# RWKV scan: inverses by 16x16 lanes joined on TensorE, the join handed out over the steps of the running chain

## The chip, the cores and the metric

One core of a Trainium2 chip runs the whole program in one launch. Five engines work side by side, each through its own queue in order: TensorE (PE, with its weight loads PEld), VectorE (DVE), ScalarE (ACT), GpSimd (POOL) and SyncE (SP), which issues the DMAs. They meet through semaphores. The metric is device time of the launch in microseconds (us); less is better.

## The reference

Two layers work on 256 context and 512 latent tokens of width 1024. Layer 0 is windowed attention with an MLP. Layer 1 is a bidirectional RWKV-7 mixer with an MLP. The change touches only the mixer's scan, which is, for 16 heads of 64 channels and for two directions:

```python
def wkv_scan(r, w, k, v, a, b, s0, reverse):
    # S_t = S_{t-1} diag(w_t) + (S_{t-1} a_t) b_t^T + v_t k_t^T ;  y_t = S_t r_t
    def step(s, inp):
        r_t, w_t, k_t, v_t, a_t, b_t = inp
        sa = jnp.einsum('bhvk,bhk->bhv', s, a_t)
        s = s * w_t[:, :, None, :] + sa[..., None] * b_t[:, :, None, :] + v_t[..., None] * k_t[:, :, None, :]
        return s, jnp.einsum('bhvk,bhk->bhv', s, r_t)
s_fwd, yc_fwd = wkv_scan(rc, decc[0], kc, vc, nac, bc, zero, False)   # context first
_, y_fwd = wkv_scan(r, dec[0], k, v, na, b, s_fwd, False)             # latents start from its state
```

The backward direction is the same with `reverse=True`. The outputs are normalised per head, gated, summed and multiplied by `w_o`.

## The kernel before

The scan is done in chunks of 64 tokens. Inside a chunk the recurrence is a triangular system, so per chunk, head and direction the kernel inverts a 64x64 unit triangular matrix, and from chunk to chunk only the 64x64 state is carried.

**Six iterations** (`its`): context for heads 0 to 7 (iteration 0), two latent iterations of four heads each (1, 2), then the same for heads 8 to 15 (3, 4, 5). A context chain has four steps, a latent chain eight. The products of an iteration are in `AR`, `BK` and `GM`, of which there are two sets, used in turn.

**Work of one iteration n.**
- `prep` (by parts of one head pair and direction: four parts for latents, eight for context): loads features, two exponentials on ACT (`en`, `cs`; one buffer for `en`), products `ko`, `bo`, `ao` and, for latents, the one with `r`. Of these `ao` is on DVE (L1201), the others on POOL (L1199, L1200, L1203). Then `grams(..., 0)`: ACT fills `pad`, PE multiplies into `g_ps` (L1224), DVE masks into `GM` (L1230).
- `lanes` (L1264): the two 32x32 diagonal blocks of every triangle are copied to `MT` (two of the four copies on POOL), transposed to `lane`, and inverted by 30 steps of forward substitution on DVE, each step in two or three streams of one product (L1281) and one sum (L1284), on all blocks at once. Each step reads what the step before wrote.
- `merge` (L1286): two transposes on DVE (L1289 to `MT`, L1292 to `dt`), then PE makes the off-diagonal 32x32 block in two rounds, `mg1` (L1299) and `mg2` (L1307), each followed by copies on ACT.
- `late`: the second half of the grams (latents), `to_end` (a product over `BK` on POOL, L1245) and `turn` (32 transposes on PE, L1323).
- `chain` (L1343): per step PE makes `x_ps` (L1368, L1371), ACT copies it to `xsb`, PE makes `u_ps` (L1394), ACT copies it to `z`, PE makes `s_ps` (L1409), and DVE adds it to the state (L1416). The state had been multiplied by its decay before, on POOL (L1387). Latents also make `y_ps` (L1426, L1430). Two groups of heads go through a step one behind the other.
- `readout`: norm, gates and bonus; its products are shared by POOL and DVE (tables `RO`, `RL`).

**Order.** The program is written as: `front(1)`, chain 0, `front(2)`, chain 1, and so on. `front(n)` is `merge(n-1)`, `prep(n)`, `lanes(n)`, and puts `late(n)` into a list `rest`; `after(i)` takes pieces of `rest` behind step i of the running chain, by the tables `LS` and `LC`. So merge n-1 has to be done before chain n-1 begins. A scheduler places all instructions on their engines by priority (earlier in the program first) and by its own estimate of when they are ready; on the chip each engine keeps that order. `prep(0)` and `lanes(0)` run beside the projections ahead of the scan. Merge 0 puts its second transpose into a free part of `GM`, since `dt` lies in memory that opens only behind the projections.

## Time and profile before

| | us |
|---|---|
| median of 3 runs | 2300.29 (2295.81 to 2302.07) |
| profiled execution, its own time | 2301.24 |
| its span, first to last instruction | 2299.5 |
| PE busy | 2052.4 (89%) |
| DVE busy | 1300.0 (57%) |
| ACT busy | 853.0 (37%) |
| POOL busy | 514.4 (22%) |

The scan takes the stretch from about 1389 to 1894 us of the span. In a row of groups the columns are line, engine, operation, output and inputs, shape, count, then busy us and mean ns of one, then idle time of the engine before them and what ended it. In a row of the timeline they are the start, the duration of the merged run, and in brackets the idle time before. An `x128` of PE there counts entries of the trace, of which each f32 matmul with a small tile makes two. PEclk is the granted share of the TensorE clock.

### The profile page before, as it was taken

Reading aid. Unit: us, or ns where it says so; the run is one execution under the profiler, and the core shown is the slowest. Engines: PE = TensorE matmul, PEld = TensorE weight load, DVE = VectorE, ACT = ScalarE, POOL = GpSimd, SP = SyncE. Lnnn points to the kernel's source line nnn. Section 1 sums busy time; section 2 is a strip of 40 time slices with the busy share of each in tenths; the row PEclk is TensorE's granted clock in tenths of the full one; section 3 lists DMA queues with packets and bytes.
Section 4 is the critical chain, followed back from the end, with each engine's and each line's share of the span. In section 5 each row is a group of like instructions: output and inputs, shape, how many; then the busy total and the mean of one; then the engine's idle time right before and its main releaser. Section 6 shows DMA issues by size and latency. Waiting matters only on the chain. (4 is left out here: it accounts for less than half of the span.)

```text
span 2299.5 us, 40632 instructions
## 1 busy us (share of the span) xinstructions
PE 2052.4 (89%) x16208; PEld 1676.3 (73%) x16208; DVE 1300.0 (57%) x2492; ACT 853.0 (37%) x1696; POOL 514.4 (22%) x586
## 2 busy tenths in 40 slices
PE   5989999989999999995989897488767996999999
PEld 4876756868888888884856786376656764788887
DVE  4455564364333343349687464985897747444444
ACT  4345454231111111116454346366655543222121
POOL 1122232010000000003011225537553332101110
PEclk9999999989999999997989898697787997999999
DMA  8244464222212222121245434203221322323322
GB/s 296 88 136 146 156 201 157 74 78 64 65 56 64 65 65 65 51 65 58 84 182 215 147 113 138 61 12 96 77 67 42 112 69 74 101 92 97 96 92 78
DMA packets 115885, 229.67 MB, mean 100 GB/s; under 512 B 12912, under 2 KB 31088, under 8 KB 115312
## 3 DMA queue, kind: packets, MB, share of 16 engines
q1 hardware_dynamic: 115696, 227.08, 30.7%
q8 instruction: 128, 2.10, 0.4%
q14 instruction: 61, 0.50, 0.1%
HBM read 191.80 MB, written 32.60 MB: 98 GB/s over the span
## 5 line engine op out<-in xcount | busy, mean ns | idle before, releaser
L337 DVE TENSOR_TENSOR wlo<-wraw,whi 128x1024 fp32r<-128x1024 f32 (+1 forms) x121 | 134.2, 1118 | 316.7 <-ACT whi L334 170.4
L362 PE MATMUL w_ps<-mhh,whi 128*128 128x512 f32 (+1 forms) x768 | 235.6, 361 | 7.4 <-POOL whi L336 4.0
L364 PE MATMUL w_ps<-mhl,whi 128*128 128x512 f32 (+1 forms) x768 | 235.6, 361 | 5.7 <-DVE mhl L317 5.7
L366 PE MATMUL w_ps<-mhh,wlo 128*128 128x512 f32 (+1 forms) x768 | 235.7, 361 | 4.1 <-DVE wlo L337 4.1
L364 PE MATMUL w_ps<-hid,w2h 128*128 128x512 f32 (+1 forms) x768 | 233.9, 359 | 0.0
L362 PE MATMUL w_ps<-hid,w2h 128*128 128x512 f32 (+1 forms) x768 | 231.1, 355 | 0.6 <-DVE X L709 0.6
L366 PE MATMUL w_ps<-hid,w2l 128*128 128x512 f32 (+1 forms) x768 | 231.1, 355 | 0.0
L336 POOL TENSOR_SCALAR whi<-wraw 128x1024 fp32r<-128x1024 f32 (+1 forms) x60 | 70.6, 1177 | 637.1 <-PE w_ps L364 261.1
L334 ACT ACTIVATE w2h<-w2raw 128x512 fp32r<-128x512 f32 x64 | 40.4, 632 | 331.2 <-PE w_ps L364 292.4
L362 PEld LDWEIGHTS w_ps<-mhh,whi 128*128 128x128 f32 x768 | 128.2, 190 | 32.1 <-POOL whi L336 4.7
L658 DVE SCALAR_TENSOR_TENSOR X<-w_ps,ada,X 128x256 f32<-128x256 f32 (+1 forms) x128 | 73.1, 613 | 137.5 <-PE w_ps L366 137.5
L364 PEld LDWEIGHTS w_ps<-mhl,whi 128*128 128x128 f32 x768 | 127.8, 190 | 31.6 <-DVE mhl L317 8.4
L366 PEld LDWEIGHTS w_ps<-mhh,wlo 128*128 128x128 f32 x768 | 127.7, 190 | 30.2 <-DVE wlo L337 7.2
L366 PEld LDWEIGHTS w_ps<-hid,w2l 128*128 128x128 f32 x768 | 127.4, 189 | 23.3
L334 ACT ACTIVATE whi<-wraw 128x1024 fp32r<-128x1024 f32 (+1 forms) x61 | 59.0, 968 | 225.4 <-PE w_ps L364 106.2
L362 PEld LDWEIGHTS w_ps<-hid,w2h 128*128 128x128 f32 x768 | 125.6, 188 | 22.9 <-issue 1.0
L364 PEld LDWEIGHTS w_ps<-hid,w2h 128*128 128x128 f32 x768 | 126.5, 188 | 20.9
L336 POOL TENSOR_SCALAR w2h<-w2raw 128x512 fp32r<-128x512 f32 x64 | 42.3, 660 | 425.9 <-PE w_ps L364 326.7
L687 ACT ACTIVATE mrelu<-w_ps 128x768 f32<-128x768 f32 (+1 forms) x64 | 44.5, 697 | 187.5 <-PE w_ps L366 187.5
L1224 PE MATMUL g_ps<-pad,bk 128*128 128x128 f32 x640 | 97.0, 306 | 16.3 <-DVE lane L1284 6.5
L1281 DVE TENSOR_TENSOR ltmp<-lane 128x36 f32<-128x36 f32 (+34 forms) x402 | 111.0, 313 | 0.1
L1284 DVE TENSOR_TENSOR lane<-lane,ltmp 128x36 f32<-128x36 f32 (+34 forms) x402 | 105.9, 301 | 0.0
(378 smaller groups left out, 4713.7 us busy)
## 6 DMA issues: line engine op xcount, KB each, us to landing
ada_w<-ada_w SPq DMA_DIRECT2D x192, 256.0 KB, 3.4
wraw<-w SPq DMA_DIRECT2D x64, 512.0 KB, 3.2
w2raw<-w SPq DMA_DIRECT2D x128, 256.0 KB, 2.7
feat<-cs SPq DMA_DIRECT2D x16, 390.0 KB, 2.4
cs<-feat SPq DMA_DIRECT2D x24, 260.0 KB, 3.5
wraw<-wq SPq DMA_DIRECT2D x8, 512.0 KB, 4.0
wraw<-wo SPq DMA_DIRECT2D x8, 512.0 KB, 3.3
wraw<-wkv SPq DMA_DIRECT2D x8, 512.0 KB, 3.4
```

What stands on the lines that cost most here:

```text
L334: nc.scalar.activation(hi, raw, AF.Copy)
L336: nc.gpsimd.tensor_scalar(hi, raw, 1.0, 0.0, ALU.mult, ALU.add)
L337: nc.vector.tensor_tensor(lo, raw, hi.bitcast(F32), ALU.subtract)
L362: nc.tensor.matmul(o, wh, cut(xh, sl), start=start, stop=False)
L364: nc.tensor.matmul(o, wh, cut(xl, sl), start=False, stop=False)
L366: nc.tensor.matmul(o, wl, cut(xh, sl), start=False, stop=stop)
L658: self.nc.vector.scalar_tensor_tensor(self.X[:, m, sl], ps[:, sl], self.ada[:, u, m, s:s + 1], self.X[:, m, sl], ALU.mult, ALU.add)
L687: nc.scalar.activation(r, ps[:, 0:n], AF.Relu)
L1224: nc.tensor.matmul(g[:, P * k:P * k + P], it.BK[:, d, b + k], pv[:, :, k], start=True, stop=True)
L1281: nc.vector.tensor_tensor(tmp, Lt[:, t0:t1, s_:s_ + 1].to_broadcast([P, m, n]), Lt[:, s_:s_ + 1, c0:c1].to_broadcast([P, m, n]), ALU.mult)
L1284: nc.vector.tensor_tensor(x, x, tmp, ALU.add)
```

## The change

**Lanes of 16.** `lanes` inverts the four 16x16 diagonal blocks of a 64x64 triangle in 14 steps instead of 30, in two streams (`q`) of a product and a sum, 56 operations of at most 56 elements per partition. All four copies to `MT` are now on ACT and DVE.

**Join on PE.** `merge` first joins pairs of 16x16 blocks to 32x32: a transpose of the upper half (L1270), a transpose of `lane` to `dt` (L1271), one round of 128 matmuls `mh1` (L1275), two copies on ACT (one of them of the new constant `half`), a second round of 128 matmuls `mh2` (L1283), a copy on ACT (L1284), and a transpose of `dt` to `MT` on DVE (L1285). Then `mg1` and `mg2` follow as before. `DT` is always `dt`.

**Where the merge stands.** `merge(n)` is now the last piece of `rest` of `front(n)`, so it belongs to the last steps of chain n-1; merge 0 stands ahead of `front(1)`. `rest` is shared out evenly over the steps from step 1 on.

**POOL to DVE.** All products of `prep`, `to_end` and `readout` go to DVE. The decay of the state is no longer a separate product: the update is one operation `state * decay + s_ps` on DVE per head pair and direction, 128x128 each (L1402), four per step of a latent chain and eight of a context chain, instead of two additions.

The diff, cut:

```diff
-LS = (0, 0, 1, 1, 1, 1, 1, 0)
-LC = (0, 2, 4, 4)
-TE = "pp"
...
-FC = 'apap'
-BC = 'pvav'
+FC = 'avav'
+BC = 'avav'
...
-                nc.gpsimd.tensor_tensor(ko, kp, en, ALU.mult)
-                (nc.gpsimd if "b" in PM else nc.vector).tensor_tensor(bo, bp, en, ALU.mult)
-                (nc.gpsimd if "a" in PM else nc.vector).tensor_tensor(ao, kk, ep[:, :, exc], ALU.mult)
+                nc.vector.tensor_tensor(ko, kp, en, ALU.mult)
+                nc.vector.tensor_tensor(bo, bp, en, ALU.mult)
+                nc.vector.tensor_tensor(ao, kk, ep[:, :, exc], ALU.mult)
                 if it.lat:
-                    nc.gpsimd.tensor_tensor(ar[:, :, 64:128], src[fl, "r"], ep[:, :, inc], ALU.mult)
+                    nc.vector.tensor_tensor(ar[:, :, 64:128], src[fl, "r"], ep[:, :, inc], ALU.mult)
...
-            nc.gpsimd.tensor_tensor(x, x, it.PC[:, ::1 - 2 * d, fl, d].unsqueeze(2).to_broadcast([P, it.nch, P]), ALU.mult)
+            nc.vector.tensor_tensor(x, x, it.PC[:, ::1 - 2 * d, fl, d].unsqueeze(2).to_broadcast([P, it.nch, P]), ALU.mult)
...
             nc.vector.transpose(lane, MT.rearrange("p u t -> p t u"))
-
             nc.vector.memset(lane[:, ::33], 1.0)
-            for s_ in range(1, 31):
+            nc.vector.memset(Lt[:, 16:32, 0:16], 0.0)
+
+            for s_ in range(1, 15):
                 jobs = []
-                for i, (t0, t1, c0, c1) in enumerate(streams(s_)):
-                    m, n = t1 - t0, c1 - c0
-                    tmp = sa.tile([P, (120, 200, 80)[i]], F32, tag=f"lt{i}", name="ltmp")[:, :m * n].rearrange("p (t i) -> p t i", t=m)
-                    x = Lt[:, t0:t1, c0:c1]
+                for q in range(2):
+                    m, n, o = 15 - s_, s_, 16 * q
+                    tmp = sa.tile([P, 56], F32, tag=f"lt{q}", name="ltmp")[:, :m * n].rearrange("p (t i) -> p t i", t=m)
+                    x = Lt[:, o + s_ + 1:o + 16, o:o + n]
                     jobs.append((x, tmp))
-                    nc.vector.tensor_tensor(tmp, Lt[:, t0:t1, s_:s_ + 1].to_broadcast([P, m, n]),
-                                            Lt[:, s_:s_ + 1, c0:c1].to_broadcast([P, m, n]), ALU.mult)
+                    nc.vector.tensor_tensor(tmp, Lt[:, o + s_ + 1:o + 16, o + s_:o + s_ + 1].to_broadcast([P, m, n]),
+                                            Lt[:, o + s_:o + s_ + 1, o:o + n].to_broadcast([P, m, n]), ALU.mult)
                 for x, tmp in jobs:
                     nc.vector.tensor_tensor(x, x, tmp, ALU.add)
 
         def merge(it):
 
             GM = it.GM
-            nc.vector.transpose(MT.rearrange("p u i -> p i u"), Lt.rearrange("p t s -> p s t"))
-
-            DT = dt if it.n else GM[:, 0, :, 64:96]
+            DT = dt
+            J = [(slice(32 * j, 32 * j + 32), j // 2, 32 * (j % 2), (32 * j, 32 * j)) for j in range(4)]
+            nc.vector.transpose(MT.rearrange("p u i -> p i u")[:, 0:16], Lt.rearrange("p t s -> p s t")[:, 0:16])
             nc.vector.transpose(DT.rearrange("p u t -> p t u"), lane)
+            ps = gtile("mh1")
+            for u in range(32):
+                for r, d, c, tp in J:
+                    nc.tensor.matmul(ps[r, 16 * u:16 * u + 16], GM[r, d, u, c:c + 32], MT[r, u, 0:16],
+                                     start=True, stop=True, tile_position=tp)
+
+            nc.scalar.activation(MT[:, :, 16:32], half.unsqueeze(1).to_broadcast([P, 32, 16]), AF.Copy)
+            nc.scalar.activation(MT[:, :, 0:16], ps.rearrange("p (u i) -> p u i", u=32), AF.Copy)
+            ps = gtile("mh2")
+            for u in range(32):
+                for r, d, c, tp in J:
+                    nc.tensor.matmul(ps[r, 16 * u:16 * u + 16], MT[r, u], DT[r, u, 16:32], start=True, stop=True, tile_position=tp)
+            nc.scalar.activation(DT[:, :, 16:32], ps.rearrange("p (u i) -> p u i", u=32), AF.Copy)
+            nc.vector.transpose(MT.rearrange("p u t -> p (u t)"), DT.rearrange("p u t -> p (u t)"))
...
-                                nc.vector.tensor_tensor(DS[g], sps, DS[g], ALU.add)
-                                sn = DS[g]
+
+                                sn = sp.tile([P, ng, 2, P], F32, tag=f"snl{g}", bufs=2, name="sn") if it.lat else S_[g]
+                                for f in range(ng):
+                                    for d in range(2):
+                                        nc.vector.scalar_tensor_tensor(sn[:, f, d], S_[g][:, f, d], it.PC[:, i, ng * g + f, d:d + 1],
+                                                                       sps[:, f, d], ALU.mult, ALU.add)
...
-                    eng(ro[2 + d]).tensor_tensor(y, y, gts[d], ALU.mult)
-                eng(ro[0]).tensor_tensor(gts[0], gts[0], gts[1], ALU.add)
-                eng(ro[1]).tensor_tensor(bv, bv, gts[0], ALU.mult)
+                    nc.vector.tensor_tensor(y, y, gts[d], ALU.mult)
+                nc.vector.tensor_tensor(gts[0], gts[0], gts[1], ALU.add)
+                nc.vector.tensor_tensor(bv, bv, gts[0], ALU.mult)
...
         def front(n):
-            if n > M0:
-                merge(its[n - 1])
             for p in prep(its[n]):
                 p()
             lanes(its[n])
-            rest.extend(late(its[n]))
-            for _ in range(LPRE):
-                if rest:
-                    rest.pop(0)()
+            rest.extend(late(its[n]) + [lambda: merge(its[n])])
 
...
         pending, rest = [], []
+        merge(its[0])
         front(1)
         for n, it in enumerate(its):
             def after(i):
                 if i % it.spb == it.spb - 1:
                     lookahead()
-                for _ in range(lper if n == len(its) - 1 else (LS if it.lat else LC)[i]):
+
+                for _ in range(TPER if n == len(its) - 1 else -(-len(rest) // (it.nch - i)) if i else 0):
                     if rest:
                         rest.pop(0)()
```

On DVE, behind the transpose that feeds merge 0, in the kernel before (`ar` is the output of `ao`, `l_...` are loaded features, `sn` is the state):

```order
L1289 STREAM_TRANSPOSE mt<-lane 128x32x32
L1292 STREAM_TRANSPOSE gm_10993<-lane 128x32x32
L1253 COPY gm_10993<-gm_10993 32x32x32 x2
L1053 TENSOR_TENSOR bv<-vT,bv_ps 128x512
L1327 COPY bk_10992<-bkt_ps 128x512
...
L1086 CAST s_gbsel<-sr_gbsel 128x512
L1201 TENSOR_TENSOR ar_12136<-l_kk,cs 128x8x64
L1414 COPY sn<-s_ps 128x512
```

The same place in the changed kernel:

```order
L1271 STREAM_TRANSPOSE dt<-lane 128x32x32
L1073 CAST s_gbsel<-sr_gbsel 128x512
L1186 TENSOR_TENSOR bk_12021<-l_kp,en 128x8x64
...
L1188 TENSOR_TENSOR ar_12020<-l_kk,cs 128x8x64
L1190 TENSOR_TENSOR ar_12020<-l_r,cs 128x8x64
L1187 TENSOR_TENSOR bk_12021<-l_bp,en 128x8x64
L1285 STREAM_TRANSPOSE mt<-dt 128x1024
L1240 COPY gm_10993<-dt 32x32x32 x2
```

The last transpose of merge 0 (L1285) stands behind nine products of `prep(1)` (two whole parts and the first product of the third), where before all DVE work of merge 0 stood ahead of `prep(1)`.

On PE, from the end of chain 0 to the beginning of chain 1, in the kernel before (`mg_` are the rounds of merge 1):

```order
L1394 MATMUL u_ps<-xsb,gm_10993 64x64 x8
L1409 MATMUL s_ps<-z,bk_10992 64x64 x6
L1323 MATMUL bkt_ps<-ident,bk_12137 128x128 x8
L1409 MATMUL y_ps<-z,bk_10992 64x64 x8
L1299 MATMUL mg_13052<-mt,gm_12138 32x32 x32
L1299 MATMUL mg_13087<-mt,gm_12138 32x32 x32
L1307 MATMUL mg_13122<-dt,mt 32x32 x32
L1307 MATMUL mg_13157<-dt,mt 32x32 x32
L1224 MATMUL g_ps<-pad_10996,bk_10992 128x128 x4
L1368 MATMUL x_ps<-z,gm_12138 64x64 x2
```

The same place in the changed kernel (`mh_` are the rounds of the join):

```order
L1391 MATMUL s_ps<-z,bk_10992 64x64 x6
L1275 MATMUL mh_13096<-mt,gm_12022 32x16 x17
L1391 MATMUL y_ps<-z,bk_10992 64x64 x2
...
L1275 MATMUL mh_13096<-mt,gm_12022 32x16 x105
L1283 MATMUL mh_13227<-dt,mt 32x16 x128
L1292 MATMUL mg_13358<-mt,gm_12022 32x32 x32
...
L1300 MATMUL mg_13463<-dt,mt 32x32 x32
L1211 MATMUL g_ps<-pad_10996,bk_10992 128x128 x4
L1361 MATMUL x_ps<-z,gm_12022 64x64 x2
```

Merge 1 still stands as one block between the two chains, now with 256 matmuls of the join ahead of its two old rounds. For merge 4, between chains 3 and 4, it is the same.

On PE inside chain 1, the changed kernel (merge 2):

```order
L1275 MATMUL mh_14274<-mt,gm_10993 32x16 x9
L1391 MATMUL s_ps<-z,bk_12021 64x64 x2
L1376 MATMUL u_ps<-xsb,gm_12022 64x64
L1275 MATMUL mh_14274<-mt,gm_10993 32x16 x2
L1376 MATMUL u_ps<-xsb,gm_12022 64x64 x3
L1361 MATMUL x_ps<-z,gm_12022 64x64 x2
L1275 MATMUL mh_14274<-mt,gm_10993 32x16 x14
L1364 MATMUL x_ps<-sn,ar_12020 64x128
L1361 MATMUL x_ps<-z,gm_12022 64x64 x2
L1275 MATMUL mh_14274<-mt,gm_10993 32x16 x3
```

In the latent chains 1, 2 and 4 the rounds of the join are cut into pieces between the chain's own matmuls: 20, 20 and 22 pieces.

## Rows read from the trace of the kernel before

**Rows 1.** Stretches of the scan: chains, and what lies between them, busy time by engine.
```profile
core 0: us, PE busy (x) PEld busy (x) DVE busy (x) ACT busy (x) POOL busy (x), PEclk, DMA share, GB/s
1397.50:1462.50 65.00, 46.85 (x592) 41.48 (x592) 44.26 (x101) 39.75 (x89) 41.67 (x41) 0.84 0.33 101
1462.50:1495.70 33.20, 9.50 (x264) 8.91 (x264) 26.68 (x73) 9.56 (x15) 15.49 (x14) 0.50 0.27 81
1495.70:1578.00 82.30, 68.51 (x1128) 59.64 (x1128) 60.14 (x183) 52.74 (x142) 42.27 (x55) 0.90 0.14 41
1578.00:1639.00 61.00, 51.77 (x775) 42.26 (x774) 47.70 (x151) 39.47 (x112) 34.93 (x41) 0.86 0.22 68
1639.00:1655.90 16.90, 9.39 (x265) 8.88 (x265) 12.36 (x26) 9.69 (x16) 12.77 (x14) 0.50 0.37 109
1655.90:1712.00 56.10, 49.77 (x601) 40.20 (x602) 46.23 (x106) 37.06 (x82) 31.99 (x29) 0.91 0.27 80
1712.00:1747.30 35.30, 9.57 (x276) 9.00 (x271) 29.30 (x75) 9.55 (x15) 17.25 (x19) 0.53 0.25 77
1747.30:1827.00 79.70, 71.77 (x1224) 60.98 (x1223) 58.99 (x183) 53.24 (x146) 28.04 (x33) 0.97 0.15 50
```
**Rows 2.** Waits of PE, 1389 to 1990: us in total, times, longest.
```profile
PE mg L1299 <- DVE mt L1289: 58.5, 4, 26.8
...
PE g_ps L1224 <- DVE lane L1284: 6.5, 3, 3.0
PE x_ps L1371 <- DVE sn L1416: 6.3, 5, 2.3
...
PE s_ps L1409 <- DVE sn L1416: 5.1, 8, 1.6
```
**Rows 3.** Groups of the lanes on DVE, from the page (all shapes of a line together).
```profile
L1281 DVE TENSOR_TENSOR ltmp<-lane 128x36 f32<-128x36 f32 (+34 forms) x402 | 111.0, 313 | 0.1
L1284 DVE TENSOR_TENSOR lane<-lane,ltmp 128x36 f32<-128x36 f32 (+34 forms) x402 | 105.9, 301 | 0.0
```
**Rows 4.** Groups on DVE by shape: masked gram, state's addition, merge's transpose, one lane product.
```profile
L1230 DVE TENSOR_TENSOR gm<-g_ps,s_gmask 128x512 f32<-128x512 f32 x80 | 54.0, 682 | 47.5 <-PE g_ps L1224 47.4
...
L1416 DVE TENSOR_TENSOR sn<-s_ps,sn 128x256 f32<-128x256 f32 x56 | 23.2, 414 | 16.1 <-PE s_ps L1409 16.0
...
L1289 DVE STREAM_TRANSPOSE mt<-lane 128x1024 f32<-128x1024 f32 x6 | 12.4, 2060 | 0.2
...
L1281 DVE TENSOR_TENSOR ltmp<-lane 128x56 f32<-128x56 f32 x18 | 2.8, 204 | 0.0
```
**Rows 5.** Stretches of merges 1 and 5, tile mg alone: PE, PEld, ACT, PEclk.
```profile
1485.00:1494.00 9.00, 7.50 (x256) 7.12 (x256) 4.12 (x8) 0.50 0.31 97
1800.00:1813.00 13.00, 6.07 (x256) 4.99 (x256) 3.51 (x6) 1.00 0.09 24
```
**Rows 6.** Group on ACT: a copy of a whole PSUM bank.
```profile
L1325 ACT ACTIVATE bk<-bkt_ps 128x512 f32<-128x512 f32 x42 | 23.8, 596 | 18.2 <-PE bkt_ps L1323 17.4
```
**Rows 7.** Timeline of PE from merge 1 to chain 1.
```profile
1485.50 3.62 PE L1299 MATMUL mg<-mt,gm 32*32 32x32 f32 x128 [26.80 <-DVE mt L1289]
1489.45 3.91 PE L1307 MATMUL mg<-dt,mt 32*32 32x32 f32 x128 [0.33 <-ACT mt L1302]
...
1495.71 0.58 PE L1368 MATMUL x_ps<-z,gm 128*64 128x64 f32 x3
```
**Rows 8.** Timeline of PE: the first matmuls of chain 0.
```profile
1397.47 1.42 PE L1368 MATMUL x_ps<-z,gm 128*64 128x64 f32 x16 [1.91 <-DMA sr_gbsel<-rconsts]
```
**Rows 9.** Timeline of POOL: first product of the third part of prep(1).
```profile
1414.83 1.27 POOL L1200 TENSOR_TENSOR bk<-l_bp,en 128x512 f32<-128x512 f32 x1 [0.45 <-ACT en L1186]
```
**Rows 10.** Group on POOL: a product of prep.
```profile
L1199 POOL TENSOR_TENSOR bk<-l_kp,en 128x512 f32<-128x512 f32 x16 | 23.3, 1455 | 20.8 <-ACT en L1186 10.5 <-DMA l_kp<-feat 10.2
```
**Rows 11.** Timeline of PE in chain 1: a piece of merge 2 behind a y_ps run.
```profile
1553.00 0.29 PE L1430 MATMUL y_ps<-ar,sn 128*64 128x64 f32 x4
1553.21 0.62 PE L1299 MATMUL mg<-mt,gm 32*32 32x32 f32 x26
```

More of the change, by code (lines that the diff above doesn't have):

```diff
@@ L82, in rconst_layout @@
     names = [("gmask", 256), ("sel", 8 * 32), ("bsel", 8 * 128), ("gsel", 4 * 32), ("gbsel", 4 * 128),
-             ("cen", 128), ("blk", 128)]
+             ("cen", 128), ("blk", 128), ("half", 16)]
     off, out = 0, {}
@@ L130, in rconst_pack @@
     put("cen", np.eye(P, dtype=np.float32) - blk / 64)
+    put("half", np.tile(np.eye(32, dtype=np.float32)[:, 16:32], (4, 1)))
     put("blk", blk)
@@ L1253, in copy @@
                 nc.vector.tensor_copy(o, i)
-        def streams(s_):
-            t, e = s_ + 1, 32
-            if s_ >= S3:
-                b = [s_ * i // C3 for i in range(C3 + 1)]
-                return [(t, e, b[i], b[i + 1]) for i in range(C3)]
-            b = [t] + [x for x in (C1 if s_ < S1 else (22,) if s_ < 20 else (27,)) if x > t] + [e]
-            return [(b[i], b[i + 1], 0, s_) for i in range(len(b) - 1)]
         def lanes(it):
@@ L1358, in chain @@
                     Z = it.zw[i // it.spb][:, :, o:o + nh]
-                    SN, DS = [None] * NG, [None] * NG
+                    SN = [None] * NG
                     for g in range(NG):
@@ L1376, in chain @@
                             nc.scalar.activation(xsb[o, d, gs], xv[o], AF.Copy)
-                        if not first and not last:
-                            DS[g] = sp.tile([P, ng, 2, P], F32, tag=f"snl{g}", bufs=2, name="sn") if it.lat else S_[g]
-                            pcb = it.PC[:, i, ng * g:ng * g + ng].unsqueeze(3).to_broadcast([P, ng, 2, P])
-                            if TE[it.lat] == "a":
-                                for f in range(ng):
-                                    for d in range(2):
-                                        nc.scalar.activation(DS[g][:, f, d], S_[g][:, f, d], AF.Copy,
-                                                             scale=it.PC[:, i, ng * g + f, d:d + 1])
-                            else:
-                                (nc.gpsimd if TE[it.lat] == "p" else nc.vector).tensor_tensor(DS[g], S_[g], pcb, ALU.mult)
                     for g in range(NG):
@@ L1465, in out @@
                 last = it.n == 5
-                eng = lambda e: nc.gpsimd if e == "p" else nc.vector
-                ro = RL if last else RO
                 bv = sp.tile([P, S], F32, tag="f4", bufs=NF4, name="bvl")
@@ L1484, in out @@
                     if d == 0:
-                        eng(ro[4]).tensor_tensor(y, y, bv, ALU.add)
-                eng(ro[5]).tensor_tensor(YT[:, 0, fl], YT[:, 0, fl], YT[:, 1, fl], ALU.add)
+                        nc.vector.tensor_tensor(y, y, bv, ALU.add)
+                nc.vector.tensor_tensor(YT[:, 0, fl], YT[:, 0, fl], YT[:, 1, fl], ALU.add)
                 if f < 4:
@@ L1518, in lookahead @@
                 values(*nx)
-        yield prep(its[0]) + [lambda fl=fl, d=d: to_end(its[0], fl, d) for fl in range(4) for d in range(2)] + [lambda: turn(its[0]), lambda: lanes(its[0])] + ([lambda: merge(its[0])] if M0 else [])
+        yield prep(its[0]) + [lambda fl=fl, d=d: to_end(its[0], fl, d) for fl in range(4) for d in range(2)] + [lambda: turn(its[0]), lambda: lanes(its[0])]
         self.pst.close()
@@ L1534, in rwkv_scan @@
         gbsel = rload("gbsel", sp, F32R).rearrange("p (i m) -> p i m", i=4)
+        half = rload("half", sp)
         geps = sp.tile([P, 1], F32, name="geps")
@@ L1625, in rwkv_scan @@
             if n == len(its) - 1:
-                tl = tail_list()
-                for _ in range(TPRE):
-                    tl.pop(0)()
-                lper = TPER
-                rest.extend(tl)
-            else:
-                lper = LPER
+                rest.extend(tail_list())
             if not it.lat:
@@ L1641, in rwkv_scan @@
                 front(n + 2)
-            elif n + 1 < len(its):
-                merge(its[n + 1])
             pending = readout(it) if it.lat else []
```

11 lines of the change are left out of this document (removed).

## The prediction

> **What bounds the kernel now.** I read the page's busy shares first: PE is busy for 89% of the span, so outside the scan, which the change leaves alone, nothing moves. Then I cut the scan into its chains and what lies between them [rows 1]. Two stretches between chains stand out: 33.2 us with PE busy for 9.5, and 35.3 us with PE busy for 9.6. The waits of PE say why: its longest is for the transpose that feeds a merge, 58.5 us in four waits, the longest 26.8 [rows 2]. That transpose waits for the lanes, 804 small operations on DVE that take 111.0 + 105.9 us, 36 us per iteration [rows 3]. So three merges (1, 3, 4) stand at a wait of DVE; merges 2 and 5 come ready inside a running chain. In the chains PE is busy for 46.9 of 65.0 us (chain 0), 68.5 of 82.3 (1), 51.8 of 61.0 (2), 49.8 of 56.1 (3) and 71.8 of 79.7 (4) [rows 1]: there PE is near its bound, and what is put on it has little room.
>
> **Part 1: lanes of 16.** They leave 56 operations per iteration in place of 134. A product of 56 columns takes 204 ns, while those of 36 columns and all others together average 301 to 313 [rows 3, 4]; at 0.20 us the lanes take 11 us instead of 36. The 58.5 us of waits then go, whatever comes in their place. What comes is the join.
>
> **Part 2: the join.** Each merge gains two rounds of 128 matmuls, 256 entries of the trace each. The trace has no 32x16 matmul; the nearest are the 256 entries of a merge, 7.50 us at the half clock (PEclk 0.50, that is 1.2 GHz) and 6.07 at the full one (2.4 GHz) [rows 5]. So 512 entries cost 12.1 to 15.0 us, or 6.0 if the time went with the columns, which are half as many; I take 12.1, since PE now comes to a merge straight from a chain. With them come two ACT copies of a bank in a row with PE, 0.60 each [rows 6], four hand-offs of about 0.33 [rows 7], and the transpose L1285, 2.06 [rows 4] (the copy of `half` and the first two transposes lie beside other work). That is 16.7 us from the first matmul of a join to its last transpose. From a merge's first old matmul to the first one of the next chain it is 1495.71 - 1485.50 = 10.2 us as before [rows 7]. A merge that stands between two chains thus takes 27 us from chain to chain (20.8 to 29.8).
>
> Between chains 0 and 1 and between 3 and 4 it stands there alone (the order of PE shows it as one block): 33.2 becomes 27, 35.3 becomes 27, so **-6.2** and **-8.3**. Most of the removed wait is given back by the join that takes its place.
>
> **Part 3: merge 0.** Before, chain 0 began at 1397.5 [rows 8], with the merge hidden in the end of the projections. Now L1285 stands on DVE behind nine products of prep(1), the ninth the first product of its third part. On POOL that one began at 1414.83 [rows 9], held by the single buffer `en` and by loads. Two parts ahead of it cost four products of 0.68 on DVE [rows 4] (the masked gram as the nearest) instead of three of 1.27 on POOL, so it comes some 2.2 us sooner: 1412.6. With the product (0.68), the transpose (2.06) and 10.2 to the first `x_ps`, chain 0 begins at 1425.5, 28.0 later; behind L1285 on PE stand the grams of prep(1) and all of chain 0. Part of this comes back: chain 0 idled for 18.1 us beside prep(1) [rows 1], which is then nearly done; with the 6.3 us of idle that chain 3 shows it gets 11.8 shorter. **+16.2.** If L1285 were not held by the products, the delay would be 16.7 and the term +4.9; if the idle stays, +28.
>
> **Part 4: joins inside chains 1, 2 and 4.** The rounds go in pieces between the chain's matmuls. Each adds 12.1 us to PE, whose idle time there is 13.8, 9.2 and 7.9 us [rows 1]; but the chain's own waits are short and not where the pieces stand, so I let half the idle time hide them: +5.2, +7.5, +8.1. Then the next chain waits for the last copy, L1285 and their hand-offs, 0.60 + 2.06 + 0.66 = 3.3 each. In chain 2 the wait of 6.7 (16.9 between the chains less 10.2) goes. Sum **+8.5, +4.1, +11.4**. All hidden: 3.3, -0.5 and 7.5; nothing hidden: 15.4, 8.7 and 15.4.
>
> **Part 5: the state.** A latent step adds two heads' groups in 0.414 each [rows 4]; now two operations of 128x128 each. The trace has none of that shape; it lies between 0.204 (56 columns) and 0.414 (256 columns); I take 0.26, so 0.1 more per group: 7 steps x 2 x 0.1 in four chains is 5.6, and for context chains (four of 0.26 for one of 0.68, two groups, three steps, two chains) 4.3. **+9.9** (from 0, if the update has slack, to 20). The product on POOL that goes ran ahead of need.
>
> **Part 6: DVE freed, POOL freed.** POOL's products of 1.46 us [rows 10] become 0.68 on DVE, and PE's other waits for DVE shrink: 6.5 us behind the lanes wholly, and half of 6.3 + 5.1 behind the state [rows 2]. **-12.2** (0 to -25). DVE's total hardly moves: about 25 us per iteration leave, and about 20 come (12 products of 0.68, four longer ones, two copies, the readout's).
>
> **Sum:** -6.2 + 16.2 + 8.5 + 4.1 - 8.3 + 11.4 + 9.9 - 12.2 = +23.4. On the profiled execution, 2301.24 (span 2299.5 and 1.7 around it), that is 2324.6; the median of the runs is 0.95 lower, so **2323**. All low ends together give -37 (2264), all high ends +79 (2380).
>
> The change of the tile's size has a rule against it. In chain 1 a piece of a merge began at 1553.21 while the run before it lasted until 1553.29 [rows 11]: no gap is seen where 32x32 matmuls follow 128x64 ones. The Trainium skill, "TensorEngine Tiling (Array Packing)", section "Key Properties", says that a change of the tiling mode, not of the tile alone, drains the engine. By the row the sum needs no term for it; by the rule every piece costs two drains, which is the fourth case below. A second rule, in the same page's "Instruction Overhead", gives each matmul about 60 cycles whatever its columns: that is 25 ns at 2.4 GHz, as an estimate 12.8 us for 512 entries against my 12.1, and the row's 23.7 ns per entry agrees.
>
> **The rivals.**
> - *The join hides, and what stays is the wait that went.* For it: PE idles 18.1, 13.8, 9.2 and 7.9 us in the chains, the join has no fixed place in a latent chain, and POOL no longer holds prep. Against it: in context chains it has nothing to hide behind. With all low ends: 2264. It decides if more than two thirds of the joins in the latent chains fall into idle time and merge 0 isn't held by prep.
> - *DVE's queue becomes the bound* (slower than the forecast). The 24 or 16 products of prep and the long ones of `to_end` now stand in one queue with the state's update, which releases the next step. If two of three of the 68 updates (34 steps, two groups) wait for one product of 0.68, it is 31 us more: 2355. For it: the chains are latency-bound at their ends. Against it: DVE is busy for 325.7 of 429.5 us even now, all stretches of rows 1 added, and PE waits for the state's update 11.4 us in all [rows 1, 2].
> - *The tiling mode drains.* 62 pieces of the join in three chains, two changes each. If a change costs the 0.29 us of the run at 1553.00, it is 36 us; at half of it 18: 2342. Rows 11 speak against it.
>
> **How the numbers follow.** The forecast has 0.47, its own range 2305 to 2342; the hidden join 0.28, spread from 2250 to 2292; DVE's queue 0.17; the drains 0.08. A measurement here can tell about 0.3% (7 us) from no change. Faster comes from the hidden join and hardly from the forecast: 0.28; within 0.3% from the two edges, 0.11; slower 0.61. The range that leaves out a tenth on each side goes from 2262 to 2362.
>
> **What would show it.** Right: the wait of PE for a merge's transpose falls from 58.5 us to the time of a join's hand-offs; `mh1` and `mh2` take 5 to 7.5 us each where they stand alone; chain 0 begins between 1414 and 1428; between chains 0 and 1 and 3 and 4 it is 24 to 30 us; lanes take under 75 us in all. Wrong: chain 0 beginning before 1410, blocks of under 20 us between the chains, or latent chains that get shorter in spite of the pieces, would mean that the join hides and that the kernel is faster; DVE waits of over 1 us ahead of most `s_ps` or `x_ps` would mean that its queue decides.

## The result, and the profile after

The changed kernel takes 2311.01 us (median of 7 runs, 2306.03 to 2318.64) against 2300.29 of before in the same comparison: a ratio of 1.0051, 95% interval 1.0035 to 1.0066, slower by about 11 us. The profiled execution took 2311.33, its span 2309.6.

The stretches of the scan, cut at the first `x_ps` of each chain and at the last matmul of chains 0, 2 and 3 (columns as in [rows 1]):

```profile
1423.60:1467.00 43.40, 41.73 (x667) 36.95 (x668) 35.26 (x105) 31.53 (x74) 3.14 (x7) 0.98 0.07 21
1467.00:1494.40 27.40, 14.45 (x716) 13.80 (x703) 12.42 (x24) 12.97 (x20) 4.29 (x6) 0.55 0.40 118
1494.40:1574.00 79.60, 71.94 (x1601) 63.28 (x1600) 47.65 (x140) 53.47 (x141) 5.57 (x14) 0.86 0.15 43
1574.00:1638.20 64.20, 58.82 (x1219) 47.78 (x1222) 47.41 (x134) 41.83 (x119) 4.84 (x10) 0.98 0.26 73
1638.20:1661.80 23.60, 14.96 (x393) 11.34 (x391) 16.18 (x25) 14.11 (x23) 2.15 (x4) 0.50 0.41 123
1661.80:1708.40 46.60, 45.53 (x589) 38.81 (x588) 38.59 (x106) 35.47 (x80) 3.12 (x6) 0.90 0.20 58
1708.40:1740.30 31.90, 16.74 (x777) 15.94 (x777) 14.97 (x32) 11.19 (x18) 5.45 (x6) 0.56 0.30 94
1740.30:1813.10 72.80, 68.75 (x1569) 60.26 (x1570) 38.95 (x115) 46.27 (x125) 4.33 (x8) 0.90 0.05 14
```

Chain 0 starts 26.1 us later than before, at 1423.6, but takes 43 us in place of 65, with PE busy for 41.7 of them, so chain 1 starts 1.3 us sooner (1494.4, [rows 7]: 1495.71). From the first `x_ps` of each chain to that of the next:

| | before | after | difference |
|---|---|---|---|
| chain 0 and merge 1 | 98.2 | 70.8 | -27.4 |
| chain 1 | 77.1 | 79.6 | +2.5 |
| chain 2 and merge 3 | 83.1 | 87.7 | +4.6 |
| chain 3 and merge 4 | 91.4 | 78.5 | -12.9 |
| chain 4 | 65.9 | 72.8 | +6.9 |
| chain 5, to the last `var_ps` | 82.8 | 84.4 | +1.6 |

(In [rows 1] the stretch of chain 4 reaches 14 us into chain 5, which begins at 1813.1 in both traces.) With the +26.1 that is +1.4: the last `var_ps` matmul begins at 1895.9 before and at 1897.5 after. The rest is lost *behind* the scan, 403.6 us before and 412.0 after, in a part whose instructions are the same but for three products of the readout, which stand on DVE instead of POOL. From here on *scan* is the time from the last `vt_ps` matmul of the projections to the last `var_ps`, and *outside* what is left of the span. Before: 509.4 and 1790.1. After: 512.0 and 1797.6.

The waits of PE in the scan (us, times, longest), which answer to [rows 2], and on DVE the lanes, a product of prep and the state's update ([rows 3, 4]):

```profile
PE mg L1292 <- DVE mt L1285: 21.9, 6, 9.4
PE mh L1283 <- issue: 12.4, 7, 2.7
PE mh L1283 <- ACT mt L1279: 10.9, 4, 6.8
PE mh L1275 <- issue: 7.2, 3, 3.6
...
PE mh L1275 <- DVE mt L1270: 6.2, 2, 6.0
```
```profile
L1260 DVE TENSOR_TENSOR ltmp<-lane 128x14 f32<-128x14 f32 (+6 forms) x168 | 27.1, 196 | 0.0
L1263 DVE TENSOR_TENSOR lane<-lane,ltmp 128x14 f32<-128x14 f32 (+6 forms) x168 | 26.7, 193 | 0.0
...
L1186 DVE TENSOR_TENSOR bk<-l_kp,en 128x512 f32<-128x512 f32 x16 | 11.0, 687 | 16.0 <-ACT en L1173 16.0
...
L1402 DVE SCALAR_TENSOR_TENSOR sn<-sn,pc,s_ps 128x128 f32<-128x128 f32 x136 | 40.6, 339 | 32.7 <-PE s_ps L1391 32.2
```

The lanes went from 217 to 54 us. The 58.5 us of waits became some 59 spread over the join and the merge: 21.9 for the last transpose, 23.3 ahead of `mh2`, 13.4 ahead of `mh1`.

Merge 1, which stands alone between chains 0 and 1, on PE and on ACT (timeline: start, duration, idle time before):

```profile
1468.58 1.49 PE L1275 MATMUL mh<-mt,gm 32*32 32x16 f32 x126 [0.99 <-issue]
1476.82 3.61 PE L1283 MATMUL mh<-dt,mt 32*32 32x16 f32 x256 [6.76 <-ACT mt L1279]
1485.64 3.46 PE L1292 MATMUL mg<-mt,gm 32*32 32x32 f32 x122 [5.20 <-DVE mt L1285]
```
```profile
1468.03 0.64 ACT L1174 ACTIVATE cs<-cs 128x520 f32<-128x520 f32 x1
1474.79 0.63 ACT L1173 ACTIVATE en<-cs 128x512 f32<-128x512 f32 x1 [6.12 <-DMA cs<-feat]
1475.51 0.64 ACT L1174 ACTIVATE cs<-cs 128x520 f32<-128x520 f32 x1
1476.17 0.60 ACT L1279 ACTIVATE mt<-mh 128x512 f32<-128x512 f32 x1
1478.81 0.63 ACT L1173 ACTIVATE en<-cs 128x512 f32<-128x512 f32 x1 [2.04 <-DMA cs<-feat]
...
1482.45 0.64 ACT L1150 ACTIVATE en<-cs 128x520 f32<-128x520 f32 x1 [2.29 <-DMA cs<-feat]
1483.18 0.64 ACT L1151 ACTIVATE cs<-cs 128x520 f32<-128x520 f32 x1
1483.72 0.58 ACT L1284 ACTIVATE dt<-mh 128x512 f32<-128x512 f32 x1
```

The rounds are short, 4.8 us (1465.29 to 1470.07, in pieces) and 3.6. The granted clock falls from 1.00 to 0.50 at 1469.8, so the first runs at the full clock and the second at the half one. But each copy of the join stands in ACT's queue behind exponentials of prep(2) that wait for a load. The first could start at 1470.1 and starts at 1476.17; the second could start at 1480.4 and starts at 1483.72. That is 9.4 of the 27.4 us between the chains. Taking the copies out of that queue was not tried.

At merge 4 PE stops inside the rounds, behind some 120 to 130 entries each time:

```profile
1719.98 1.83 PE L1275 MATMUL mh<-mt,gm 32*32 32x16 f32 x121 [3.63 <-issue]
...
1724.15 1.90 PE L1283 MATMUL mh<-dt,mt 32*32 32x16 f32 x128 [1.36 <-issue]
1727.62 1.84 PE L1283 MATMUL mh<-dt,mt 32*32 32x16 f32 x122 [1.57 <-issue]
```

*issue* is time in which the engine waited for nothing that the profile shows; such waits of the join come to 12.4 + 7.2 us in the scan. The DMA packets of the trace tell what they most likely are. The queue q8 carries instructions in packets of 16 KB, and the page counts them (packets, MB, share), before and after:

```profile
q8 instruction: 128, 2.10, 0.4%
```
```profile
q8 instruction: 152, 2.49, 0.5%
```

The 24 more are the 6 x 1024 instructions of the join (512 entries and their weight loads in each merge), 256 to a packet. At merge 4 packets of this queue land at 1718.53, 1722.70 and 1726.11, and PE goes on at 1719.98, 1724.15 and 1727.62, 1.5 us behind each. All ten stops on issue of the join in the scan end 1.3 to 1.5 us behind such a landing, and so do all ten in the second profile (after_again). PE gets through the 128 entries of a packet in 1.9 us here, while the packets land 3.4 to 4.2 us apart: `mh2` takes 7.0 us (1722.49 to 1729.46) for 4.0 us of work. A round of `mg` takes some 3.5 us for as many entries at this clock, about the pace of the packets. That PE waits for its instructions is read from these times; no run changes their number alone.

### The profile page after: what moved, and what is told of

Same layout as the page of the kernel before. It is cut to its first block, busy times and chain, and to the rows that moved or that the text cites. A ratio compares the mean times of both kernels' runs of the same rounds, so it can differ in the third digit from the quotient of the medians.

```text
span 2309.6 us, 46213 instructions
## 1 busy us (share of the span) xinstructions
PE 2098.6 (91%) x19280; PEld 1711.7 (74%) x19280; DVE 1241.5 (54%) x2280; ACT 868.5 (38%) x1720; POOL 277.1 (12%) x360
## 5 line engine op out<-in xcount | busy, mean ns | idle before, releaser
L1211 PE MATMUL g_ps<-pad,bk 128*128 128x128 f32 x640 | 98.2, 305 | 3.2 <-ACT pad L1208 1.8
L1211 PEld LDWEIGHTS g_ps<-pad,bk 128*128 128x128 f32 x640 | 85.3, 210 | 12.0 <-ACT pad L1208 5.7
L550 DVE CUSTOM_DVE_ANT_0 sm<-sc_ps,consts,vecs 128x256 f32<-128x256 f32 (+2 forms) x96 | 71.7, 760 | 39.4 <-PE pt_ps L571 20.5
## 6 DMA issues: line engine op xcount, KB each, us to landing
wraw<-w SPq DMA_DIRECT2D x64, 512.0 KB, 3.6
wraw<-wq SPq DMA_DIRECT2D x8, 512.0 KB, 4.4
wraw<-wo SPq DMA_DIRECT2D x8, 512.0 KB, 3.6
wraw<-wkv SPq DMA_DIRECT2D x8, 512.0 KB, 3.6
```

The source lines that it names most:

```text
L550: nc.vector.tensor_tensor_reduce(sm[:, :nk], ps[:, :nk], self.c["band"][:, b0:b0 + nk], rs[:, h:h + 1], self.v["sink"][:, hd:hd + 1], ALU. ...
L1211: nc.tensor.matmul(g[:, P * k:P * k + P], it.BK[:, d, b + k], pv[:, :, k], start=True, stop=True)
```

## The experiments

Times are medians; the ratio is to the kernel before in the same comparison, whose median was 2298.4, 2298.3 and 2298.2 in the three sets. The last two columns are of the run's one profile, which need not lie near the median (products_back 2313.0, lanes32_prod_back 2279.9, merge_front 2303.3), so differences of a few us between them tell nothing. *16* stands for lanes of 16 with the join, *rest* for the merge handed out, *prod* for the products of prep and `to_end` on DVE, *state* for the new update. Where *prod* is missing in a run derived from the changed kernel, the readout's products and the copies stay on DVE and ACT.

| run | parts | us | ratio (95%) | scan | outside |
|---|---|---|---|---|---|
| before | none | 2300.3 | 1 | 509.4 | 1790.1 |
| state_alone | state | 2291.0 | 0.9973 (0.9963 to 0.9983) | 498.0 | 1788.9 |
| lanes32_prod_back | rest, state | 2286.6 | 0.9946 (0.9928 to 0.9964) | 495.5 | 1782.6 |
| lanes32_state | rest, prod | 2290.9 | 0.9967 (0.9955 to 0.9980) | 500.9 | 1784.3 |
| lanes32 | rest, prod, state | 2297.5 | 0.9993 (0.9982 to 1.0005) | 505.2 | 1787.4 |
| lanes16_alone | 16 | 2322.5 | 1.0096 (1.0079 to 1.0114) | 523.1 | 1799.3 |
| prod_state | 16, rest | 2308.1 | 1.0043 (1.0030 to 1.0056) | 513.7 | 1790.7 |
| products_back | 16, rest, state | 2303.5 | 1.0023 (1.0010 to 1.0037) | 512.9 | 1798.0 |
| state_back | 16, rest, prod | 2299.3 | 1.0003 (0.9994 to 1.0013) | 500.3 | 1797.3 |
| merge_front | 16, prod, state | 2309.0 | 1.0045 (1.0028 to 1.0062) | 510.6 | 1790.9 |
| merge0_early | all, merge 0 moved up | 2307.2 | 1.0044 (1.0027 to 1.0061) | 511.0 | 1793.6 |
| changed kernel | all | 2311.0 | 1.0051 (1.0035 to 1.0066) | 512.0 | 1797.6 |
| after_again | all | 2307.6 (one) | | 508.6 | 1797.2 |

**lanes32**: the changed kernel with `streams`, `lanes` and `merge` of the kernel before (`DT = dt` throughout).

> The changed kernel with the lanes of 32 and without the join; all else of the change stays (merge in the rest of the front, products and state's update on DVE). Theory 1 (the join gives back what the lanes gain): without it chain 0 begins some 12 us sooner (1410), chains 1, 2 and 4 lose what the pieces cost, and the lanes, on a DVE that no POOL products slow, take 804 operations of about 0.21 us, 28 us per iteration and not 36, so the blocks between chains 0 and 1 and 3 and 4 are 20 to 28 us; in all 10 to 25 us below the changed kernel, 2286 to 2301. Theory 2 (the join hides, the time is lost elsewhere): the waits for the lanes come back at 58 us and the time is at or above that of the changed kernel, 2311 to 2335.

13.5 us faster than the changed kernel, as theory 1 had it, by the profiles 5 of it in the scan and the rest outside. The working held only in part: the waits for the lanes are back, and 38 and 37 us lie between the chains (1452.3 to 1490.1, 1700.2 to 1737.1), not 20 to 28. Chain 0 begins at 1396.6, 27 us before that of the changed kernel, and yet chain 1 only 4.3 us earlier. What held is the lanes' duration. The wait of PE, and the lanes on DVE:

```profile
PE mg L1290 <- DVE mt L1280: 57.9, 4, 27.3
```
```profile
L1272 DVE TENSOR_TENSOR ltmp<-lane 128x36 f32<-128x36 f32 (+34 forms) x402 | 76.7, 228 | 0.0
L1275 DVE TENSOR_TENSOR lane<-lane,ltmp 128x36 f32<-128x36 f32 (+34 forms) x402 | 76.2, 228 | 0.0
```

The same 804 operations took 111.0 + 105.9 us in [rows 3].

**products_back**, in the changed kernel:
```diff
-nc.vector.tensor_tensor(ko, kp, en, ALU.mult)
+nc.gpsimd.tensor_tensor(ko, kp, en, ALU.mult)
```
and the same for `bo`, the product with `r` and `to_end`.

> The changed kernel with three of four products of prep and the long product of to_end back on POOL. Theory 1 (the products on DVE shorten what runs beside them: chain 0 took 41.7 us after and 65.0 before, and a product on DVE took 0.69 after and 0.98 before): chain 0 takes 55 to 65 us again, DVE's own products 0.9 to 1.0, and the time is 10 to 25 us above the changed kernel, 2321 to 2336. Theory 2 (the products had slack on POOL, and chain 0 is short because it begins 26 us later, when prep is done): chain 0 stays below 48 us and the time is within 7 us of 2311.

Both wrong: 7.5 us faster. (The 41.7 us in theory 1 is PE's busy time in chain 0; the chain took 43.4.) The slow-down of DVE is there (a 128x512 product of `ao` 1.22 us in place of 0.69, lane operations 0.25 in place of 0.19), chain 0 takes 48.5 us, but the time falls.

**state_back**, in the changed kernel:
```diff
+DS[g] = sp.tile(...) if it.lat else S_[g]
+nc.gpsimd.tensor_tensor(DS[g], S_[g], pcb, ALU.mult)
...
-nc.vector.scalar_tensor_tensor(sn[:, f, d], S_[g][:, f, d], it.PC[...], sps[:, f, d], ALU.mult, ALU.add)
+nc.vector.tensor_tensor(DS[g], sps, DS[g], ALU.add)
```

> The changed kernel with the state's decay back as one product on POOL and one addition on DVE. Theory 1 (the forecast's term: two operations of 0.34 in the step's path for one of 0.41): the time falls by about 10 us, to 2301. Theory 2 (the update has slack: PE waits for it 1.0 us in the changed kernel and waited 11.4 before): no change or up to 10 us longer, 2311 to 2321, and PE's waits for the state's update go up to some 10 us.

11.7 us faster, theory 1, and all of it in the scan (500.3 against 512.0 and 508.6). PE's waits for the state are short in both, so the time does not come back there by name. The wait of `mh1` for the transpose of the lanes, of those that changed, over the scan (6.2 us in the changed kernel):

```profile
PE mh L1275 <- DVE mt L1270: 2.7, 2, 2.0
```

That the longer updates hold up what stands behind them on DVE fits this. At merge 1 the wait of `mh2` for its copy is 2.4 in place of 6.8 us, but a stop on issue of 2.4 us comes in its place, and over the scan the waits for this copy are the same (10.8 and 10.9 us). The path of the rest of the 11.7 us is not shown.

**merge_front**, in the changed kernel: `merge(its[n - 1])` at the head of `front(n)`, none in `rest`.

> The changed kernel with merge(n) at the head of the next front, as before, and not in the rest that is handed out over the chain. Theory 1 (handed out, a join costs 3 to 10 us in a latent chain; as one block it stands between the chains): the chains 1, 2 and 4 get 3 to 10 us shorter each, and the stretches behind them 15 to 27 us longer: 2330 to 2365. Theory 2 (the scheduler places the pieces by readiness whatever the place in the program): within 7 us of 2311.

Theory 2. The chains shift among themselves (chain 2 with merge 3 takes 11 us less, chains 1, 3 and 4 4 to 5 more each), the sum does not change. With all these products on DVE, handing the merge out brings and costs nothing that shows.

**state_alone**: the edit of state_back, reversed, in the kernel before.

> The kernel before with the state's update alone changed: no product on POOL, two or four scalar_tensor_tensor on DVE. Taking this part back out of the changed kernel gave 11.5 us. Theory 1 (the longer update lies in the path of every step, whatever else the kernel does, as the forecast's +9.9 had it): 2306 to 2311. Theory 2 (it costs only where DVE carries the products as well): within 4 us of 2298. POOL loses some 50 us of work by it, so the lanes on DVE should come down from 0.32 us an operation to about 0.30, which gives back 1 to 2 us in front of merges 1, 3 and 4.

Neither: 7.3 us *faster* than before, where theory 1 had it slower. The by-remark holds: lane operations 0.29 us, not 0.31 (100.9 + 97.5 us).

**lanes16_alone**: `lanes` and `merge` of the changed kernel, and the constant `half`, in the kernel before.

> The kernel before with lanes of 16 and the join, and nothing else of the change: merge at the head of the next front, products and state as before. In the changed kernel the lanes of 16 with the join are 13 us slower than lanes of 32. Theory 1 (the join costs more than the waits that it removes, on any DVE): 2305 to 2315. Theory 2 (beside POOL's products a lane operation takes 0.32 us and not 0.23, so leaving 78 of 134 of them away is worth 25 us a front here and 15 there, and the join wins or draws): 2285 to 2300.

Theory 1, and beyond it: 24 us slower, 14 of them in the scan.

**lanes32_state**: the edits of lanes32 and state_back together.

> The changed kernel with lanes of 32 without the join, and with the state's decay back on POOL: what stays of the change is the products on DVE and the merge in the rest. Each of the two alone gave 13 and 11.5 us. Theory 1 (they lie in different places, one between the chains and in their pieces, one in each step, and add up): 2283 to 2290. Theory 2 (both make room for the same waits, so the second is worth little): 2293 to 2299.

Just above the range of theory 1: of 13.5 + 11.7 us, 20 add up.

**prod_state**: the edits of products_back and state_back together.

> The changed kernel with three products of prep, the long product of to_end and the state's decay back on POOL: what stays is the lanes of 16 with the join and the merge in the rest. Each of the two alone gave 7.5 and 11.5 us. Theory 1 (they add up): 2290 to 2294. Theory 2 (POOL slows DVE when it works beside it, so the second costs back what the first gave): 2297 to 2304.

Beyond theory 2: either one put back gains, both put back give the kernel of 2308. With lanes of 16 in the rest, moving the products alone is worth -9 us (2308.1 to 2299.3), the state alone -5 (to 2303.5), the second of them +7.5 or +11.7. With lanes of 32 in the rest it is the same: from *state* to both +10.9 (2286.6 to 2297.5), from *prod* to both +6.6 (2290.9 to 2297.5). One load off POOL pays, the second costs; where it costs is not shown. The largest step is another: from lanes16_alone to prod_state, -14.4 us (2322.5 to 2308.1), which hands the merge out and takes the readout's products and two copies of the lanes off POOL. These were not separated; one difference is that PE changes to or from 32x32 tiles 234 times in the scan there and 174 times here, at 0.11 to 0.15 us or more.

**pool_beside**, in the kernel of lanes32, ahead of the lanes of front 1 and later:
```diff
+for _ in range(20 if it.n else 0):
+    nc.gpsimd.tensor_tensor(dum, GM[:, 0, 0:16, 0:32], GM[:, 1, 0:16, 32:64], ALU.mult)
```

> The kernel of run lanes32 (lanes of 32 and no join, products and state on DVE, 2297.5 us) with 20 products of 128x512 on POOL beside the lanes of each front from the second on; they read the masked grams and write a tile that nothing reads, so they add work to POOL and none to DVE or PE. Theory 1 (work on POOL stretches DVE's operations that run beside it): the mean of a lane operation goes from 0.23 us back to 0.30 or more while they run, a front's lanes get some 8 to 12 us longer, the waits of PE for a merge's transpose grow from 58 to 70 us or more, and the time is 8 to 30 us above 2297.5. Theory 2 (POOL does not touch DVE; the lanes got shorter because fewer other operations stand between them): lane operations stay at 0.23 and the time within 5 us of 2297.5.

Theory 1, by more than it said: +64 us, 2361.4. Operations on DVE, and POOL in the same stretch (a run of several is merged in a line):

```profile
1730.36 1.11 DVE L1403 SCALAR_TENSOR_TENSOR sn<-sn,pc,y_ps 128x128 f32<-128x128 f32 x4
1735.40 1.32 DVE L1275 TENSOR_TENSOR ltmp<-lane 128x90 f32<-128x90 f32 x1
1736.78 1.30 DVE L1278 TENSOR_TENSOR lane<-lane,ltmp 128x90 f32<-128x90 f32 x1
1738.13 0.39 DVE L1275 TENSOR_TENSOR ltmp<-lane 128x98 f32<-128x98 f32 x2
1738.44 0.39 DVE L1278 TENSOR_TENSOR lane<-lane,ltmp 128x98 f32<-128x98 f32 x2
1739.27 1.20 DVE L1275 TENSOR_TENSOR ltmp<-lane 128x104 f32<-128x104 f32 x1
```
```profile
1729.44 2.14 POOL L1267 TENSOR_TENSOR dum<-gm 128x512 f32<-128x512 f32 x1
1735.34 1.28 POOL L1267 TENSOR_TENSOR dum<-gm 128x512 f32<-128x512 f32 x1
1736.69 1.27 POOL L1267 TENSOR_TENSOR dum<-gm 128x512 f32<-128x512 f32 x1
1737.91 1.09 POOL L1330 MEMSET z<- 64x512 f32 x2
1739.08 1.27 POOL L1267 TENSOR_TENSOR dum<-gm 128x512 f32<-128x512 f32 x1
```

The lane operation that begins at 1735.40, just behind the start of a product on POOL, ends at 1736.72, 0.1 us behind the product's end; the next two that meet a product do the same, and beside memsets two take 0.39 together. Four updates of the state, whose second array is in PSUM, take 1.11 together in the middle of a product. It goes both ways: the product at 1729.44 meets a longer operation of DVE that began at 1728.31, and takes 2.14 us in place of 1.27.

Counted over the scan, a lane operation takes either up to 0.43 us, 0.22 to 0.23 on average with lanes of 32 and 0.19 to 0.20 with lanes of 16, or over 0.45. Of the slow ones there are 61 of 670 here, 1.16 us each; all began while POOL ran such an instruction, and ended 0.03 to 0.20 us behind its end. Before there are 79, 1.06 each, 77 of them of this kind. They get fewer with each load that leaves POOL: 43 in state_alone, 36 in lanes32_state, none in lanes32; 30 of 280 in lanes16_alone, 23 in prod_state, 20 in state_back, 13 in products_back, none in the changed kernel. So the second load frees lanes too, and what it costs must lie elsewhere. PE's wait for the state's update, queued behind the slow lanes:

```profile
PE x_ps L1365 <- DVE sn L1403: 29.7, 21, 3.5
```

**lanes32_prod_back**: the edits of lanes32 and products_back together.

> The kernel of run lanes32 with the products of prep and to_end back on POOL: lanes of 32 without the join, merge in the rest, the state's update on DVE. Theory 1 (of the two loads that leave POOL one is worth having, either one, and both together load DVE's queue too much; the place of the merge hardly matters): as run state_alone, 2288 to 2294. Theory 2 (the merge in the rest costs by itself, and run lanes32_state hid that): 2295 to 2301.

Below the range of theory 1, and faster than both kernels: 2286.6, 0.5% below before. The readout's products and the copies of the lanes are on DVE and ACT here too, which state_alone lacks.

**merge0_early**: `merge(its[0])` behind `lanes(its[0])` in the projections, with `DT = dt if it.n else GM[:, 0, :, 64:96]` and `half` loaded earlier.

> The changed kernel with merge 0, join included, moved up into the end of the projections, behind the lanes of front 0, so that chain 0 need not wait for the transpose behind prep(1)'s products. Theory 1 (the late beginning of chain 0, 1423.6 in place of 1397.5, is a loss that the shorter chain 0 makes good only in part): chain 0 begins before 1405, chain 1 some 5 to 15 us sooner, 2296 to 2306. Theory 2 (chain 0 is held to prep(1)'s and front 1's DVE work and ends where it did): chain 1 begins within 4 us of 1494.4, and the time stays at 2306 to 2315.

The edit did not move the work: PE still starts `mh1` at 1388.9, and the transpose still comes behind eight products of prep(1):

```profile
1412.34 0.68 DVE L1191 TENSOR_TENSOR ar<-l_r,cs 128x512 f32<-128x512 f32 x1
1412.94 1.23 DVE L1286 STREAM_TRANSPOSE mt<-gm 128x1024 f32<-128x1024 f32 x1
```

Chain 0 began at 1428.4. The time, 2307.2, is what theory 2 had, but its case was not made, so what an early chain 0 would be worth in this kernel stays open.

**after_again**: no edit.

> The changed kernel once more, unchanged, for a second profile. In the first, the scan ended only 1.6 us later than in the kernel before (last statistics matmul at 1897.5 and 1895.9), and 8.4 us were lost behind it, in a stretch whose instructions are the same in both (412.0 and 403.6 us). Theory 1 (the stretch behind the scan varies from execution to execution by when its weights arrive, and the cost of the change lies in the scan): a stretch of 402 to 407 us, and a scan that ends later than 1900 where the whole time is near 2311. Theory 2 (the change lengthens that stretch): 409 to 414 us again, with the scan's end within 3 us of 1897.5.

Between the two: 408.0 us behind the last `var_ps`, and the scan's end at 1897.8. *Outside* is 1797.2 again. Over all profiles it is 1782.6 to 1792.8 (mean 1787.7) in the six kernels without the join and 1790.7 to 1799.3 (mean 1795.6) in the eight profiles with it. Its code is nearly the same: ahead of the scan `prep(0)` and `lanes(0)` differ, behind it three of the readout's products (in lanes32 too). Behind the last `var_ps` the two groups do not overlap: 401.0 to 404.2 us without the join, 404.9 to 412.0 with it. What differs there with the join, in every profile, is how long a weight load takes. The line of the DMA issues (count, KB each, median us to landing) of before and of the changed kernel:

```profile
wraw<-w SPq DMA_DIRECT2D x64, 512.0 KB, 3.2
```
```profile
wraw<-w SPq DMA_DIRECT2D x64, 512.0 KB, 3.6
```

It is 3.2 in all six without the join and 3.5 or 3.6 in all eight with it, ahead of the scan as behind it. At one place behind the scan such a load comes late, ACT waits for it with work of PE queued behind, and PE idles 2.5 us and then runs on at half the clock (granted 0.50 from 2039.8 to 2043.2). That the loads cost the 8 us is not shown beyond this place, and why they are slower is open: `half` isn't the cause (lanes32 loads it too), nor is the chip (state_alone and lanes16_alone ran on the same one); that the program with the join is longer, and what that moves in memory, was not tested.

## Why the prediction was right, and where it was not

The side and the range were right; the size was twice too large (2323 against 2311), and more than half of what was measured is not where the sum had it. That the time came out inside the range is in good part luck: the sum of +23 for the scan became about +1, and the stretches that were to stay as they are brought +7.

- *"Outside the scan ... nothing moves"* failed. The two profiles of the changed kernel have +7.3 us outside, against +1 in the scan (512.0 and 508.6 against 509.4), where the sum had +23.4. With 7.9 us between the means of the kernels with and without the join this is more than one execution's chance, but its cause isn't shown.
- *Part 1* held: 0.19 to 0.20 us an operation, 9 us an iteration.
- *Part 2*: 27 us from chain to chain, measured 27.4 at merge 1 (-5.8, the term was -6.2) and 31.9 at merge 4 (-3.4, the term was -8.3). The size at merge 1 is right by errors that cancel. The rounds of the join there take 6.77 us of PE for 512 entries and not 12.1; the copies' 9.4 us in ACT's queue and the stops on issue, 19.6 us in all merges together, weren't in the sum:

```profile
1465.00:1481.00 16.00, 6.77 (x512) 6.19 (x512) 0.60 (x1) 0.65 0.42 124
```

  That row (columns as in [rows 5]) is 13.2 ns an entry, but it spans both clocks, since PE did not keep the full clock from the chain as the prediction took it. From start to start the entries stand 8.4 to 9.3 ns apart at the full clock (`mh1`) and 13.3 at the half one (`mh2`), where those of `mg` behind them stand 26.0 apart. So the low bound, by columns, was the right one, though the join also works in four row groups and `mg` in two, which no run separates. And the sentence falls that the trace agrees with the Trainium skill's "TensorEngine Tiling (Array Packing)", "Instruction Overhead": a fixed 60 cycles for each matmul, 25 ns as the prediction's estimate had it, would be 12.8 us. The other row of [rows 5], 29.3 ns an entry at the half clock, spoke against it from the start: 60 cycles of 1.2 GHz are 50 ns.
- *Part 3* had the delay (1423.6, forecast 1425.5) and its place, but too small a give-back, which is the largest miss inside the scan: chain 0 went from 65.0 to 43.4 us, 21.6 less and not 11.8. It idles for 1.7 us, not 6.3, at a clock of 0.98 instead of 0.84. The term of +16.2 is 26.1 - 21.6 = +4.5. Chain 3 lost 9.5 us too (56.1 to 46.6), about half of it idle time and at nearly the same clock (0.91 and 0.90), which the sum had not at all.
- *Part 4*: +2.5, +4.6 and +6.9 for +8.5, +4.1 and +11.4; the rounds were cheaper and more of them hid.
- *Part 5*: +9.9, measured 11.7 in the changed kernel by state_back, at 0.34 us an operation and not 0.26. But it is no cost of the update as such: alone it *gains* 7.3, and beside lanes of 16 without *prod* 4.6. It costs where the products are on DVE too. That is the setting of the rival of DVE's queue, but not its sign: PE waits for the state 1.0 us in all ahead of `x_ps`. By which path the two together cost is open.
- *Part 6* is not borne out as a term. The waits that it names went (6.5 + 6.3 + 5.1 us, now 1.0), but moving *prod* and *state* together costs 2.9 us (prod_state against the changed kernel), and what gains is the step from lanes16_alone to prod_state. What the prediction missed is what POOL's products do to DVE: its "804 small operations" of 0.31 us are many of 0.22 and 79 in the scan of over a microsecond on average. The Trainium skill states it, "SBUF — State Buffer", section "Who interferes with whom": a DVE instruction with two inputs in SBUF contends with a GpSimd instruction that reads SBUF, and not with one that only writes. pool_beside shows each half of it. The section calls this an exclusive lock, and the trace agrees: the slow lane operations of pool_beside ended 0.03 to 0.20 us behind the product that they met.
- Of the rivals, the hidden join happened by half in the scan. Drains of the tiling mode do show, against the reading of rows 11. The profile models when an entry ends, so a missing gap tells nothing; the starts do. In chains 1, 2 and 4, from the last 128x64 entry to the first 32x32 one it is 0.151 us or more in all 62 changes, mostly 0.152, and back 0.107 or more in all 61, mostly 0.107, while entries of one of these shapes mostly follow each other within 0.06. That is about 0.2 us a piece, 12 us of PE for the 62 pieces (an estimate from these numbers), part of it in idle time; the rival had 18 to 36, the sum nothing.

## What to carry to other kernels

Before a load is moved from POOL to DVE, ask which operations of DVE ran beside it: here those with two inputs in SBUF waited for the whole of POOL's product, 1.1 to 1.2 us in place of 0.22. That gain can still be lost: the first load that went paid 5 to 9 us, the second cost 7 to 12. Undo the parts of a bundle one at a time and in pairs: here one part gained alone and cost in company, and the version without the join, with the state's update and with the products left on POOL beats both kernels. Before work is cut into many small matmuls, count their instructions and their changes of tile shape, and not only their columns: the rounds of the join were half as long as expected, and PE stopped in them for its instructions. And when a small copy is put between two PE rounds, look at what stands ahead of it on ACT; a load that an exponential waits for holds the join.

## What was not expected of the hardware

- A two-input DVE operation on SBUF that begins beside a product on POOL ends with it (1.1 to 1.3 us), alone it takes 0.22 to 0.23; memsets on POOL leave it at 0.23 to 0.25, and an update with one input in PSUM stays at 0.33. A product on POOL that meets such a DVE operation goes from 1.27 to 2.1 us.
- PE used up 256 instructions of small matmuls in 1.9 us, while packets of as many landed 3.4 to 4.2 us apart, and stopped for 1.0 to 3.6 us each time, 19.6 us in the scan.
- 32x16 f32 entries stand 13.3 to 13.8 ns apart at the half clock and 8.4 to 9.3 at the full one; 32x32 ones 26.0 to 26.7 at the half clock. A change from 128x64 to 32x32 tiles costs 0.15 us from start to start, the change back 0.11.
- The same weight load takes 3.2 us in six kernels and 3.5 to 3.6 in eight profiles of those with the join; the stretches outside the scan take 8 us longer in these.
